# Moving stores behind their data, and reweaving two product halves, in a hybrid RG-LRU and attention block

## The chip, the cores and the metric

The kernel runs on one core of one Trainium2 chip. The metric is device time in microseconds (us) of one execution. Five engines work side by side, each in the order in which its instructions were written: TensorE (PE, with its weight loads as PEld), VectorE (DVE), ScalarE (ACT), GpSimd (POOL) and SyncE (SP), which here only issues transfers between DRAM and the on-chip memory (SBUF).

## The reference

One encoder block on x of 256 tokens by 2048 channels, in float32:

```python
xn = rms_norm(x, norm_pre_w)
z = xn @ w_in                        # 2048 x 13312
u_lru, g_lru, q, k, v, g_attn, m_lru, m_attn = split(z)
u = centred_depthwise_conv(u_lru)    # width 4
h = rg_lru(u, forward) + rg_lru(u, backward)   # gates of 128x128 blocks, then a scan over tokens
y_a = h * silu(g_lru)
y_b = windowed_gqa(rope(q), rope(k), v, sink) * silu(g_attn)
merged = sigmoid(m_lru) * (y_a @ w_proj_a) + sigmoid(m_attn) * (y_b @ w_proj_b)
out = x + rms_norm(merged @ w_out, norm_post_w)
```

## The kernel before

All weights are read once from one packed DRAM tensor, `wall`, in rows of 1 MB (128 partitions by 2048 floats). Each row is turned into two rounded pieces, a high one `wh` (a cast on ACT, L217) and the rest `wl` (a subtraction on DVE, L219), and each product is made of three matmuls on PE: high by high, high by low, low by high.

**Steps.** Three strings (START, MERGE, OUT) write out by hand the order in which rows are used. In START, `g`, `h`, `w`, `k` are blocks: `g2.0` is a row of the gates of branch A (tile `gl`), `h` of branch B (`ga`), `w` of the LRU's input (`u`), `k` of the keys, and two rows make one result. A name with `m`, such as `Lm6.0`, is a part of a product that is computed in Strassen's manner with seven products instead of eight: L and M are the two halves of the merge gate `m_lru`, and this document calls them the two gate halves. Time in the program is counted in half steps: a block takes two, a part one. START has 140 half steps. Index expressions such as `at(T, fn)` or `soon(fn, d)` put work at half step T, or d half steps from now, into every engine's order.

**What is loaded when.** `fetch` runs at the start of each step. A block's row (and the rows of `m2`) goes into a ring of three `raw` tiles, three steps ahead, by a load on SP (L205). The parts `m1`, `m5`, `m6`, `m4` of one half share two cells x of two tiles each (`Lx0a` and so on): the first is loaded and the others are added into it by accumulating loads on POOL (L190), five steps ahead; `m3` and `m7` share the cells y, and the first load of x or y goes through SP (L192), four steps ahead. A part with a sum of x as its other operand also loads that sum, 512 KB, four steps ahead (`x_sum`, L335, tile `Lm` or `Mm`). The LRU's own gate weights come four half steps ahead of each pair of blocks (L627). A block's or a part's row is split into `wh` and `wl` two steps ahead of its matmuls.

**What is put away.** SBUF doesn't hold all. It is cut into 45 tiles of 512 KB, the `units`, from which weights' pieces, LRU tiles, cells, sums and results are all drawn; a new tile waits until the last instruction on the one that it replaces is done, and the one that was given back longest ago is taken first. So results that are needed only later are stored to DRAM by `park` (L787) and read back by `back` (L791): the sigmoid gates `tm` (of L and M), the silu gates `sga`, the first branch's results `ya`, the second's `yb` and the first product `pa`. The eight groups of sums of x are computed at half steps 18, 22, ... 46 (`x_sums`) and stored too (L330, DRAM tensor `away`).

All of these stores and nearly all loads stand in one order, SP's. SP waits at each transfer until the data are there (a store), or until the place is free (a load); everything behind it in SP's order stands too. Before, the stores stand 2 or 3 half steps behind the instruction that makes their data.

Of the kernel before, what the change touches and what calls it, by code (L numbers as in the profile page):

```python
# [59 lines left out]
    o3.2 o3.3""".split()  # L60

START = """u0.0 u0.1 u0.2 u0.3 v0.0 v0.1 v0.2 v0.3 g0.0 g0.1 h0.0 h0.1 w4.0 w4.1 g2.0 g2.1 h2.0 h2.1 w6.0 w6.1 g4.0 g4.1
    Lm1.0 h4.0 h4.1 Lm1.1 w8.0 Lm2.0 w8.1 Lm2.1 g6.0 Lm5.0 g6.1 Lm5.1 h6.0 h6.1 Lm3.0 w10.0 Lm3.1 w10.1 Lm6.0 g8.0
    Lm6.1 g8.1 Lm7.0 h8.0 h8.1 Lm7.1 w12.0 Lm4.0 w12.1 Lm4.1 g10.0 Mm1.0 g10.1 Mm1.1 h10.0 h10.1 Mm2.0 w14.0 Mm2.1
    w14.1 Mm5.0 g12.0 Mm5.1 g12.1 Mm3.0 h12.0 h12.1 Mm3.1 g14.0 Mm6.0 g14.1 Mm6.1 h14.0 Mm7.0 h14.1 Mm7.1 k0.0 k0.1
    Mm4.0 k2.0 Mm4.1 k2.1""".split()
XSUM = (18, 22, 26, 30, 34, 38, 42, 46)
LRU = (-4, 0, 2, 2, 2, 2, 2, 4)
QUADS = {"u": ("w_in", U0), "v": ("w_in", V0), "p": ("w_proj_a", 0), "a": ("w_in", MA0),
# [44 lines left out]
def body(ctx, tc, x, xT, wall, wlru, pvec, npost, ident_d, mask_d, rope_d, out):  # L114
# [9 lines left out]
    def unit(name, dt=F32, shape=(P, 4, S)):  # L124
        return units.tile(list(shape), dt, tag="u", name=name)

    def bank(name, shape=(P, 2, S)):
        return psum.tile(list(shape), F32, tag="bg", name=name, bufs=4)
# [4 lines left out]
    def half_unit(name, tag, dt=F32, bufs=2):  # L133
        return small.tile([P, 2, S], dt, tag=tag, name=name, bufs=bufs)
# [10 lines left out]
    def parts_of(h, l, src):  # L145
        nc.scalar.copy(h, src)  # L146
        soon(lambda: nc.vector.tensor_tensor(l, src, h.bitcast(F32), ALU.subtract))
# [12 lines left out]
    def at(hs, fn):  # L160
        assert hs >= now[0], (hs, now[0])
        due.setdefault(hs, []).append(fn)
# [9 lines left out]
    def soon(fn, d=1):  # L172
        at(now[0] + d, fn)
# [127 lines left out]
    def sums_of(name, src, done, f=None):  # L301
        a = src.rearrange("p a b -> p (a b)")
        a11, a12, a21 = (a[:, i * P:(i + 1) * P] for i in (0, 2, 1))
        ends = src.rearrange("p a (b c) -> p (a b) c", b=2)[:, 0:4:3]
        psum = f is None
        f = (half_unit(f"{name}f", "uu", F32) if psum else f).rearrange("p a (b c) -> p (a b) c", b=2)
        t = unit(name, F32R, (P, 4, 2, P))

        def make(a21):
            nc.vector.tensor_tensor(f[:, 0:2], ends, a21.unsqueeze(1).to_broadcast([P, 2, P]), ALU.subtract)  # L310
            nc.vector.scalar_tensor_tensor(f[:, 2], f[:, 1], -1.0, a11, ALU.mult, ALU.subtract)
            nc.vector.scalar_tensor_tensor(f[:, 3], f[:, 2], -1.0, a12, ALU.mult, ALU.subtract)
            soon(lambda: parts_of(t[:, :, 0], t[:, :, 1], f))
            done(t)

        if psum:

            nc.scalar.copy(f[:, 3], a21)
            soon(lambda: make(f[:, 3]))
        else:  # L320
            make(a21)
# [5 lines left out]
    def x_sums(n):  # L327
        v = unit(f"xa{n}")
        nc.vector.tensor_tensor(v[:, 0:2], xs[n][:, :, 0].bitcast(F32), xs[n][:, :, 1].bitcast(F32), ALU.add)
        store = lambda t: nc.sync.dma_start(away[n // 4][:, :, n % 4], t.rearrange("p a b c -> p a (b c)").bitcast(F32))  # L330
        sums_of(f"xx{n}", v[:, 0:2], lambda t: soon(lambda: store(t), 3), v[:, 2:4])

    def x_sum(name, s, q):
        t = unit(name, F32R, (P, 4, 2, P))
# [283 lines left out]
    sgl, sga = [], []  # L618
    ya, yb = [None] * 8, [None] * 8

    def lru_pair(n, b):

        v = {}
# [67 lines left out]
        def gate_out():  # L691
            h = v["gr"]
            y = sgl[n // 4][:, n % 4:n % 4 + 2]
            nc.vector.tensor_tensor(h[:, 0:2], h[:, 0:2], h[:, 2:4], ALU.add)
            nc.vector.tensor_tensor(y, h[:, 0:2], y, ALU.mult)
            v.clear()
            if n in (2, 6, 10):
                soon(lambda: park("ya", sgl, n // 4), 2)
            elif n > 10:
                soon(lambda: y_parts(n // 2))  # L700

# [14 lines left out]
    def y_parts(q):  # L716
        ya[q] = pair_unit(f"ya{q}")
        n = q % 2 * 2
        parts_of(ya[q][:, :, 0], ya[q][:, :, 1], sgl[q // 2][:, n:n + 2])

    def silu_evac(units_list, n):
        def done(ps):
            if n % 4 == 0:
                units_list.append(unit(f"sg{n}"))
            dst = units_list[n // 4][:, n % 4:n % 4 + 2]

            def sigmoid():
                sg = half_unit(f"sig{n}", "p")
                nc.scalar.activation(sg, dst, AF.Sigmoid)
                soon(lambda: nc.vector.tensor_tensor(dst, dst, sg, ALU.mult))  # L730
                if units_list is sga and n % 4 == 2:
                    soon(lambda: park("sga", sga, n // 4), 3)

            scaled(dst, ps, lambda: soon(sigmoid))
        return done

    tm, sm, ms, msum = {}, {}, {}, {}
# [6 lines left out]

    def gated_out(gates, c, t):
        if t == 1 and gates is tm:
            soon(lambda: park("tm", tm, c), 2)

    def gate_evac(gates, c):
        def done(t, ps):  # L750
# [31 lines left out]
    def park(key, store, c):  # L782

        d = parked[key, c] = dram.tile([P, 1024], F32, name=f"park{key}{c}")
        t = store[c]
        store[c] = None
        nc.sync.dma_start(d, flat(t))  # L787
# [58 lines left out]
    def head(hd, qh, ql, b, both):  # L846

        g, j = hd // 4, hd % 4
        sk = pv[:, PV_SINK + hd:PV_SINK + hd + 1]
        ts = [slice(t * P, (t + 1) * P) for t in range(2)]  # L850
        v = {}

        def scores():
            v["sc"] = bank(f"sc{hd}")
            for t in range(2):
                mm3(v["sc"][:, t], qh[:, j, ts[t]], ql[:, j, ts[t]], kv["kh"][:, g], kv["kl"][:, g], True, True)

        def expo():
            p = v["p"] = half_unit(f"p{hd}", "p")
            sc = v.pop("sc")  # L860
            m, nm, es = tiny(f"m{hd}"), tiny(f"nm{hd}"), tiny(f"es{hd}")
            dn = v["dn"] = tiny(f"dn{hd}")
            for t in range(2):
                nc.vector.tensor_tensor_reduce(p[:, t], sc[:, t], table["mask"][:, t], rtok_sc[:, t:t + 1], sk, ALU.add, ALU.max, m[:, t:t + 1])  # L864
            nc.vector.tensor_scalar(nm, m, -1.0, None, ALU.mult)
            soon(lambda: exps(p, nm, es, dn))

        def exps(p, nm, es, dn):
            for t in range(2):
                nc.scalar.activation(p[:, t], p[:, t], AF.Exp, bias=nm[:, t:t + 1], accum_out=dn[:, t:t + 1])  # L870
            nc.scalar.activation(es, nm, AF.Exp, bias=sk)
            v["es"] = es

        def normalise():
            dn, rd = v["dn"], tiny(f"rd{hd}")
            nc.vector.tensor_tensor(dn, dn, v["es"], ALU.add)
            nc.vector.reciprocal(rd, dn)
            soon(lambda: [nc.scalar.activation(v["p"][:, t], v["p"][:, t], AF.Copy, scale=rd[:, t:t + 1]) for t in range(2)])

        def flip():  # L880
            v["pt"] = bank(f"pt{hd}")
            for kt in range(2):
                for t in range(2):
                    nc.tensor.transpose(v["pt"][:, kt, ts[t]], v["p"][:, t, ts[kt]], ident)  # L884

        def p_parts():
            if j % 2 == 0:
                both.update({s: unit(f"p{s}{hd}", F32R, (P, 2, 2, S)) for s in "hl"})
            parts_of(both["h"][:, :, j % 2], both["l"][:, :, j % 2], v.pop("pt"))
            v.clear()  # L890

        def values():
            both["o"] = bank(f"o{hd}")
            ks = slice(g * P, (g + 1) * P)
            for kt in range(2):
                mm3(both["o"], kv["vh"][:, kt, ks], kv["vl"][:, kt, ks], both["h"][:, kt], both["l"][:, kt], kt == 0, kt == 1)

        def gate_out():
            y = sga[g][:, j - 1:j + 1]
            nc.vector.tensor_tensor(y, both["o"], y, ALU.mult)  # L900
            both.clear()
            if j == 3 and g < 3:
                soon(lambda: park("yb", sga, g), 2)

        for d, fn in ((0, scores), (1, expo), (3, normalise), (5, flip), (6, p_parts)):
            at(b + d, fn)
        if j % 2 == 1:
            at(b + 10, values)
            at(b + 11, gate_out)
# [17 lines left out]
    def add_pa(c):  # L927
        def done(t, ps):
            nc.vector.tensor_tensor(tm[c][:, t], ps, tm[c][:, t], ALU.mult)
            if t == 1:  # L930
                soon(lambda: park("pa", tm, c), 2)

        add_rows(f"pa{c}_", ya, done)

# [94 lines left out]
    b, n = ticks(), ticks(len(plan))  # L1029
# [159 lines left out]
```

## Time and profile before

| | |
|---|---|
| median of 3 runs | 894.74 us (894.59 to 894.96) |
| the profiled execution | 894.17 us, of which 892.2 us from the first instruction to the last |
| DVE busy | 714.1 us (80%) |
| ACT busy | 611.6 us (69%) |
| POOL busy | 58.6 us (7%) |
| transfers | 235.13 MB, mean 264 GB/s |
| SP's queue, POOL's queue | 60.0% and 19.5% of the 16 DMA engines' time |
| granted TensorE clock | 0.998 |

The profile is one execution. An engine's busy time is the union of its instructions; a matmul's end is modelled, and the next one starts before it. "Releaser" is what ended a wait. A store or load is seen twice: when SP (or POOL) issues it, and when its data have landed. The DMA share of a window can read a little over 1.

### The profile page before, as it was taken

What the parts mean: (1) busy time and instruction counts of PE and PEld (TensorE: products, weight loads), DVE (VectorE), ACT (ScalarE), POOL (GpSimd) and SP (SyncE); (2) the same over time, 40 slices, a digit from 0 to 9 for tenths busy, and PEclk for the clock granted to TensorE, in tenths of its full rate; (3) what the DMA queues carried; (4) which work ended last, traced back from release to release, by engine and by line L of the source; (5) the groups of instructions that cost most, each with busy time, mean ns of one, the idle gap of its engine ahead of it and who ended that gap; (6) DMA issues with size and microseconds to landing.
All of it is one profiled execution on the core that took longest, in us unless ns stands there. A gap on an engine that the chain in (4) does not pass through costs nothing.

```text
span 892.2 us, 12273 instructions
## 1 busy us (share of the span) xinstructions
PE 879.0 (99%) x4566; PEld 753.0 (84%) x4566; DVE 714.1 (80%) x974; ACT 611.6 (69%) x885; POOL 58.6 (7%) x88
## 2 busy tenths in 40 slices
PE   9999999999899999999999999999999999999996
PEld 8888888888688888888888888888888888888885
DVE  6899999898697987898987768576676776687776
ACT  7689697869688795998554565455587654455754
POOL 0000000011001011100000000000101100000200
PEclk9999999999999999999999999999999999999999
DMA  9757689899859989965867556556999997799972
GB/s 337 261 189 265 221 290 302 292 330 288 299 195 316 314 260 321 315 212 203 313 231 259 189 189 218 188 208 239 303 327 333 304 289 255 276 316 387 230 181 95
DMA packets 51420, 235.13 MB, mean 264 GB/s; under 512 B 5377, under 2 KB 10241, under 8 KB 35105
## 3 DMA queue, kind: packets, MB, share of 16 engines
q1 hardware_dynamic: 41568, 200.03, 60.0%
q0 software_dynamic: 9216, 33.56, 19.5%
q10 hardware_dynamic: 576, 0.76, 0.3%
q8 instruction: 36, 0.59, 0.3%
q14 instruction: 24, 0.19, 0.1%
HBM read 218.60 MB, written 15.73 MB: 263 GB/s over the span
## 4 chain that ended last, share of the span: by engine, by line
PE 72%; DVE 9%; DMA 9%; issue 5%; ACT 3%; POOLq 0%; ACTq 0%; SPq 0%; DVEq 0%; POOL 0%
DMA raw<-wall_dram 9%; PE q L250 7%; DVE wl L219 5%; PE q L248 3%; PE ga L250 3%; PE gl L250 3%; PE k L250 2%; PE u L250 2%; PE ga L248 2%; ACT wh L217 2%; PE gl L248 2%; PE Am L225 1%; PE Am L223 1%; PE Am L224 1%; PE u_ps L540 1%
## 5 line engine op out<-in xcount | busy, mean ns | idle before, releaser
L219 DVE TENSOR_TENSOR wl<-raw,wh 128x1024 fp32r<-128x1024 f32 (+1 forms) x264 | 311.7, 1201 | 49.1 <-ACT wh L217 42.7
L217 ACT CAST wh<-raw 128x1024 fp32r<-128x1024 f32 (+1 forms) x263 | 264.7, 1037 | 57.6 <-DMA raw<-wall_dram 44.5
L250 PE MATMUL gl<-xs,wh 128*128 128x512 f32 x256 | 63.5, 391 | 2.3 <-ACT wh L217 2.3
L250 PE MATMUL ga<-xs,wh 128*128 128x512 f32 x256 | 63.5, 391 | 0.0
L250 PE MATMUL q<-xs,wh 128*128 128x512 f32 x256 | 62.8, 391 | 0.0
L250 PEld LDWEIGHTS gl<-xs,wh 128*128 128x128 f32 x256 | 46.9, 188 | 11.7 <-ACT wh L217 2.7
L250 PEld LDWEIGHTS ga<-xs,wh 128*128 128x128 f32 x256 | 46.7, 188 | 8.8
L250 PEld LDWEIGHTS q<-xs,wh 128*128 128x128 f32 x256 | 46.6, 188 | 8.8
L146 ACT CAST ph<-pt 128x512 fp32r<-128x512 f32 x16 | 9.4, 588 | 61.9 <-PE pt L884 61.9
L250 PE MATMUL u<-xs,wh 128*128 128x512 f32 x192 | 47.5, 391 | 0.0
L250 PEld LDWEIGHTS u<-xs,wh 128*128 128x128 f32 x192 | 35.2, 188 | 6.7
L248 PEld LDWEIGHTS ga<-xs,wl 128*128 128x128 f32 x256 | 32.9, 191 | 3.0 <-DVE wl L219 1.9
L248 PE MATMUL ga<-xs,wl 128*128 128x256 f32 x256 | 33.9, 283 | 1.3 <-DVE wl L219 1.3
L248 PE MATMUL q<-xs,wl 128*128 128x256 f32 x256 | 34.4, 284 | 0.0
L248 PEld LDWEIGHTS q<-xs,wl 128*128 128x128 f32 x256 | 33.1, 191 | 1.2
L248 PEld LDWEIGHTS gl<-xs,wl 128*128 128x128 f32 x256 | 32.8, 191 | 1.3
L248 PE MATMUL gl<-xs,wl 128*128 128x256 f32 x256 | 33.2, 283 | 0.0
L864 DVE CUSTOM_DVE_ANT_0 p<-sc,table,pv 128x256 f32<-128x256 f32 x32 | 16.1, 541 | 19.9 <-PE sc L225 19.9
L248 PEld LDWEIGHTS u<-xs,wl 128*128 128x128 f32 x192 | 24.6, 191 | 0.9
L248 PE MATMUL u<-xs,wl 128*128 128x256 f32 x192 | 24.9, 283 | 0.0
L645 DVE SCALAR_TENSOR_TENSOR uu<-upad,pv,uu 128x256 f32<-128x256 f32 x48 | 23.2, 483 | 1.7
L146 ACT CAST ms<-mt 128x512 fp32r<-128x512 f32 x8 | 4.7, 588 | 24.2 <-PE mt L950 24.2
(524 smaller groups left out, 2256.6 us busy)
## 6 DMA issues: line engine op xcount, KB each, us to landing
raw<-wall_dram SPq DMA_DIRECT2D x127, 1024.0 KB, 6.4
lraw<-wlru_dram SPq DMA_DIRECT2D x8, 512.0 KB, 5.8
away<-xx SPq DMA_DIRECT2D x8, 512.0 KB, 3.7
Lm<-away SPq DMA_DIRECT2D x8, 512.0 KB, 16.9
Mm<-away SPq DMA_DIRECT2D x8, 512.0 KB, 15.1
Am<-away SPq DMA_DIRECT2D x8, 512.0 KB, 10.1
raw<-wall_dram SPq DMA_DIRECT2D x8, 256.0 KB, 4.7
parksga<-sg SPq DMA_DIRECT2D x4, 512.0 KB, 4.7
```

What stands on the lines that cost most here:

```text
L146: nc.scalar.copy(h, src)
L217: cast(hs, raw)
L219: nc.vector.tensor_tensor(ls, raw, hs.bitcast(F32), ALU.subtract)
L223: nc.tensor.matmul(ps, wh, xh, start=start, stop=False, skip_group_check=more)
L224: nc.tensor.matmul(ps, wh, xl, start=False, stop=False, skip_group_check=more)
L225: nc.tensor.matmul(ps, wl, xh, start=False, stop=stop, skip_group_check=more)
L248: nc.tensor.matmul(ps[:, 1], wl[:, sl], a[:, 0], start=False, stop=False)
L250: nc.tensor.matmul(ps, wh[:, sl], a, start=k == 0, stop=k == KT - 1)
L540: nc.tensor.matmul(ups[b // 2][:, b % 2, m], w[:, sl], a[:, n], start=k == 0 and w is wh and m == 0, stop=stop)
L645: nc.vector.scalar_tensor_tensor(u, up[:, j, tap:tap + S], cw[:, tap:tap + 1], u, ALU.mult, ALU.add)
L864: nc.vector.tensor_tensor_reduce(p[:, t], sc[:, t], table["mask"][:, t], rtok_sc[:, t:t + 1], sk, ALU.add, ALU.max, m[:, t:t + 1])
```

## The change

Two things. First, the stores are issued later, counted in half steps behind their data: sums of x 3 becomes 7, `ya` 2 becomes 7, `sga` 3 becomes 7, `tm` 2 becomes 5, `yb` and `pa` 2 become 4. Nothing is added or taken away. Second, in START the parts of L and M are moved by one block here and there. Counted in half steps from the start, all blocks from `h6.0` on begin at the same half step or one earlier, and all parts from `Lm5.1` on at the same or two later (`Mm7.1`: four later). For example `Lm6.0 g8.0 Lm6.1 g8.1 Lm7.0 h8.0` (half steps 72 to 79) becomes `Lm6.0 g8.0 g8.1 Lm6.1 h8.0 Lm7.0` (72 to 80). Since `fetch` goes by steps and the LRU's work by the half step of its `g` block, those move along.

```diff
@@ START
-    Lm1.0 h4.0 h4.1 Lm1.1 w8.0 Lm2.0 w8.1 Lm2.1 g6.0 Lm5.0 g6.1 Lm5.1 h6.0 h6.1 Lm3.0 w10.0 Lm3.1 w10.1 Lm6.0 g8.0
-    Lm6.1 g8.1 Lm7.0 h8.0 h8.1 Lm7.1 w12.0 Lm4.0 w12.1 Lm4.1 g10.0 Mm1.0 g10.1 Mm1.1 h10.0 h10.1 Mm2.0 w14.0 Mm2.1
-    w14.1 Mm5.0 g12.0 Mm5.1 g12.1 Mm3.0 h12.0 h12.1 Mm3.1 g14.0 Mm6.0 g14.1 Mm6.1 h14.0 Mm7.0 h14.1 Mm7.1 k0.0 k0.1
-    Mm4.0 k2.0 Mm4.1 k2.1""".split()
+    Lm1.0 h4.0 h4.1 Lm1.1 w8.0 Lm2.0 w8.1 Lm2.1 g6.0 Lm5.0 g6.1 h6.0 Lm5.1 h6.1 Lm3.0 w10.0 Lm3.1 w10.1 Lm6.0 g8.0
+    g8.1 Lm6.1 h8.0 Lm7.0 h8.1 Lm7.1 w12.0 Lm4.0 w12.1 g10.0 Lm4.1 g10.1 Mm1.0 h10.0 Mm1.1 h10.1 Mm2.0 w14.0 w14.1
+    Mm2.1 g12.0 Mm5.0 g12.1 Mm5.1 h12.0 Mm3.0 h12.1 g14.0 Mm3.1 g14.1 Mm6.0 h14.0 Mm6.1 h14.1 Mm7.0 k0.0 k0.1 Mm7.1
+    k2.0 Mm4.0 k2.1 Mm4.1""".split()
@@ x_sums
-        sums_of(f"xx{n}", v[:, 0:2], lambda t: soon(lambda: store(t), 3), v[:, 2:4])
+        sums_of(f"xx{n}", v[:, 0:2], lambda t: soon(lambda: store(t), 7), v[:, 2:4])
@@ lru_pair, gate_out
-                soon(lambda: park("ya", sgl, n // 4), 2)
+                soon(lambda: park("ya", sgl, n // 4), 7)
@@ silu_evac
-                    soon(lambda: park("sga", sga, n // 4), 3)
+                    soon(lambda: park("sga", sga, n // 4), 7)
@@ gated_out
-            soon(lambda: park("tm", tm, c), 2)
+            soon(lambda: park("tm", tm, c), 5)
@@ head, gate_out
-                soon(lambda: park("yb", sga, g), 2)
+                soon(lambda: park("yb", sga, g), 4)
@@ add_pa
-                soon(lambda: park("pa", tm, c), 2)
+                soon(lambda: park("pa", tm, c), 4)
```

## The prediction

> **What bounds the kernel now.** I read the page first, for the engine that is nearly full.
>
> ```profile
> PE 879.0 (99%) x4566; PEld 753.0 (84%) x4566; DVE 714.1 (80%) x974; ACT 611.6 (69%) x885; POOL 58.6 (7%) x88
> ```
>
> TensorE is busy for 99% of the 892.2 us span, and the change gives it the same matmuls, only in another order. So a gain can only come from the moments when PE stands still, and a loss only from new ones. The view of waits, for PE alone, names them all:
>
> ```profile
> PE gl L250 <- ACT wh L217: 2.3, 1, 2.3
> PE ga L248 <- DVE wl L219: 1.3, 2, 1.1
> ...
> PE gate L223 <- ACT gi L669: 0.6, 1, 0.6
> ```
>
> What is left out stands in the first 20 us, ahead of all that is changed. PE's timeline shows where the first two rows lie:
>
> ```profile
> 226.68 0.39 PE L223 MATMUL Lm<-wh,Lm 128*128 128x512 f32 x1
> ...
> 228.94 0.39 PE L224 MATMUL Lm<-wl,Lm 128*128 128x512 f32 x1
> 229.17 0.39 PE L225 MATMUL Lm<-wh,Lm 128*128 128x512 f32 x1
> 231.85 2.12 PE L250 MATMUL gl<-xs,wh 128*128 128x512 f32 x8 [2.29 <-ACT wh L217]
> ...
> 240.28 1.97 PE L250 MATMUL ga<-xs,wh 128*128 128x512 f32 x8
> 242.46 1.22 PE L248 MATMUL ga<-xs,wl 128*128 128x256 f32 x8 [0.21 <-DVE wl L219]
> 244.73 1.21 PE L248 MATMUL ga<-xs,wl 128*128 128x256 f32 x8 [1.05 <-DVE wl L219]
> ```
>
> By the order of START these are `Lm6.1` (226.68), `g8.1` (231.85), `Lm7.0`, and `h8.0` (240.28). A matmul is shown with 0.39 us, but the next one starts 0.23 after it: modelled ends hide 0.16 us of each wait. The four waits are thus 2.29 + 0.21 + 1.05 + 0.6 = 4.15 us as shown and 4.15 + 4 x 0.16 = **4.8 us** by starts. That is the most that the change can bring. ACT's timeline tells what they waited for:
>
> ```profile
> 230.75 2.00 ACT L217 CAST wh<-raw 128x1024 fp32r<-128x1024 f32 x2 [7.25 <-DMA raw<-wall_dram]
> ...
> 237.69 1.06 ACT L217 CAST wh<-raw 128x1024 fp32r<-128x1024 f32 x1 [1.59 <-DMA raw<-wall_dram]
> ```
>
> The weights of `g8.1` landed at 230.7 and those of `h8.0` at 237.7; ACT had stood idle for 7.25 and 1.59 us. The waits on DVE at 242 and 244 are what that delay left on ACT and DVE. So I went to the transfers, by stretches:
>
> ```profile
> 170.00:175.00 5.00, 5.00 (x31) 4.45 (x31) 4.43 (x6) 4.42 (x5) 0.87 (x1) 1.00 0.41 106
> 175.00:240.00 65.00, 62.71 (x340) 54.22 (x339) 52.51 (x61) 46.97 (x64) 9.70 (x13) 1.00 1.04 314
> 310.00:315.00 5.00, 5.00 (x32) 4.43 (x31) 4.96 (x8) 4.98 (x9) 0.00 (x0) 1.00 0.42 164
> 320.00:385.00 65.00, 64.39 (x352) 55.83 (x351) 55.00 (x65) 53.43 (x70) 9.28 (x11) 1.00 1.04 313
> ```
>
> The last two columns are the DMA share and GB/s. From 175 to 240 us and from 320 to 385 the DMA engines are full, at 314 GB/s; just ahead of each stretch they are idle for more than half of 5 us. SP's timeline and its waits (window 160 to 180) show why:
>
> ```profile
> 164.06 0.33 SPq L205 DMA_DIRECT2D raw<-wall_dram  x1
> 173.08 0.33 SPq L787 DMA_DIRECT2D parkya<-sg  x1
> 173.50 0.41 SPq L205 DMA_DIRECT2D raw<-wall_dram  x1
> ```
>
> ```profile
> SPq L787 <- DVE sg L695: 8.7, 1, 8.7
> ```
>
> SP stood for 8.7 us at the store of `ya`, whose data DVE made only at 173; the next weights stood behind it. The second gap is the same with `sga`:
>
> ```profile
> 307.80 0.33 SPq L627 DMA_DIRECT2D lraw<-wlru_dram  x1
> 314.54 0.33 SPq L787 DMA_DIRECT2D parksga<-sg  x1
> ```
>
> **The change, part by part.** *The stores of `ya` and `sga`, five and four half steps later.* The row behind the first gap, that of `h6.1`, takes the ring place of `g6.0`, which was free when DVE had split it:
>
> ```profile
> 167.18 1.23 DVE L219 TENSOR_TENSOR wl<-raw,wh 128x1024 fp32r<-128x1024 f32 x1 [1.94 <-ACT wh L217]
> ```
>
> At 168.4 us, so its 1 MB can go 5.1 us earlier. It needs 1.05 MB / 314 GB/s = 3.3 us of transfer, and the gap offers 0.59 x 5 = 2.95 us. All that follows in the full stretch then lands 2.95 us earlier. The second gap offers 0.58 x 5 = 2.9 us to the stretch after 320. The store itself comes behind its data by more than SP ever waited for it, and costs no wait of its own.
>
> *The weave around half step 75.* SP issued in this order before:
>
> ```profile
> 193.82 0.33 SPq L205 DMA_DIRECT2D raw<-wall_dram  x1
> 201.98 0.33 SPq L335 DMA_DIRECT2D Lm<-away  x1
> 208.46 0.33 SPq L627 DMA_DIRECT2D lraw<-wlru_dram  x1
> 209.69 0.33 SPq L787 DMA_DIRECT2D parksga<-sg  x1
> 210.11 0.43 SPq L205 DMA_DIRECT2D raw<-wall_dram  x1
> 211.69 0.33 SPq L335 DMA_DIRECT2D Lm<-away  x1
> 212.11 7.96 SPq L205 DMA_DIRECT2D raw<-wall_dram  x2
> ```
>
> These are the rows of `g8.0` (193.82), the sum for `Lm6.1`, LRU weights, the store of `sga`, `g8.1` (210.11), the sum for `Lm7.0`, and `h8.0` with `h8.1` (212.11). The row of `g8.1` takes the place of `w10.0`, which DVE gave back at 201.3:
>
> ```profile
> 200.06 1.22 DVE L219 TENSOR_TENSOR wl<-raw,wh 128x1024 fp32r<-128x1024 f32 x1
> ```
>
> In the new order `fetch` asks for `g8.1` at half step 70, ahead of the sum for `Lm6.1` and of the other two, instead of at 72 behind all three. So it goes out at 201.3 instead of 210.1. With the same 230.7 - 210.1 = 20.6 us to landing it is there at 221.9 and cast at 223.0. PE needs it where `Lm6.1` was, at 226.7: 3.7 us in hand, and the 2.29 wait goes.
>
> What is late next is `h8.0`. Its new place: a part takes 229.17 + 0.23 - 226.68 = 2.72 us, a block 240.28 - 231.85 - 2.72 = 5.71 us, so `g8.1` and `Lm6.1` end at 226.68 + 5.71 + 2.72 = 235.1. A cast takes 1.06, so the row must land by 234.0, against 237.7 before: 3.7 us are wanted. To be had are the 2.95 us of the gap, and 1.67 us (0.52 MB / 314 GB/s) each for the store of `sga` and the sum for `Lm7.0`, which now stand behind this row on SP: 6.3 us in all, landing at 231.4. The bounds are 0 (order changes, the bytes don't) and 6.3; I take 6.3, since the gap is seen in the windows and the order follows from the code. Anything over 3.7 gives the same time. The DVE waits go along, for ACT and DVE are then not held up.
>
> *The weave around half step 118.* The gate wait came when ACT stood at the row of `g14.0`, as the chain of waits shows:
>
> ```profile
> 331.30 22.27 DMA raw<-wall_dram
> ```
>
> PE needs it one half step (2.7 us) sooner now. It gains the second gap's 2.9 us, and the first loads of the cells of `Mm3.1` with their sum (1.57 MB, 5.0 us) now go behind it instead of ahead of the rows before it; 5.2 us better in the balance, against a wait of 0.6 + 0.16. It goes; if not, 0.8 us remain.
>
> *The stores of the sums of x, `tm`, `yb` and `pa`.* SP's waits and the table of transfers:
>
> ```profile
> SPq L330 <- DVE xx L147: 39.6, 8, 8.5
> ```
>
> ```profile
> parktm<-mg SPq DMA_DIRECT2D x4, 512.0 KB, 4.4
> ```
>
> Some 5 us of SP's time per store of sums go, but PE had no wait in that stretch, so nothing is gained there. Two reads come closer behind their stores: the sum for `Lm5.1` three half steps (8.2 us) behind the last store of sums, and `tm` for `p0` two (5.4 us). The stores land in about 4.4 us, so SP stands little or not at all; what queues behind it are weights for which three ring tiles are filled ahead. I take nothing; the other end is the 1 to 2 us by which a slow landing would hold SP.
>
> *Longer use of SBUF.* Each store holds one of the 45 units for two to five half steps more, and a unit is wanted for every quarter of a block, 5.71 / 4 = 1.4 us. A load can wait for one, as the sum at 201.98 did for 7.8 us:
>
> ```profile
> SPq L335 <- PE gate L225: 8.1, 2, 7.8
> ```
>
> Such a load would then wait up to 1.4 us more, or 2.8 with two stores held at once. I take 0, since `g8.1` no longer stands behind such a load, and keep 2.8 for the range. The Trainium skill speaks against this part: "Perfetto Trace Analysis", Identifying Performance Opportunities, says that recurring gaps on the engine that should be full can mean that SBUF has no room for the next tile, and by that rule holding tiles longer lengthens the gaps. The trace bears it out only in part, since ACT's 7.25 us were ended by a DMA; what it would cost is the second rival.
>
> **The sum.** 4.8 us of waits go and nothing comes: the profiled execution's 894.17 us (892.2 of span, 2.0 around it) become 889.4. The median of the runs is 0.57 above that execution, so 894.74 - 4.8 = **889.9 us**. A measurement of this kernel can tell 0.2%, 1.8 us, from no change.
>
> **Rivals.** *Full engines stay full.* From 175 to 240 us the DMA share is 1.04, and what is issued earlier could only wait longer. For it: `h8.0` took 25.6 us to land. Against it: the 41% just before. Then `g8.1` is in time, but `h8.0` still lands at 237.7, is cast at 238.75, 3.6 us after its new place; with the DVE waits (0.21 + 1.05 + 0.32) and the gate's 0.8 the waits are 6.0 instead of 4.8 us: 895.9. The Trainium skill has the ground for this, too: "DMA: Bandwidth & Descriptors", Issuing engines are not separate DMA queues, says that all queues run on the same 16 engines.
>
> *SBUF runs short, and the kernel gets slower.* The delayed `sga` and `ya` hold units in this very stretch; SP stands longer at the sum and the LRU weights ahead of `h8.0`, which is asked for 2.8 us later and lands at 240.5. It is 6.4 us late for a place that moved forward; with 1.6 and 0.8 as above the waits are 8.8 us: 898.7. It decides from where the row of `h8.0` lands later than 238.2 (waits of 4.8 + 1.8, less 1.6 and 0.8, are 4.2 us behind 235.1, less the cast). For it: SP did stand for a unit here. Against it: one or two units are few of 45.
>
> *Half of it.* `g8.1` is in time, `h8.0` and the gate keep their waits (2.5 us): 892.4, still faster.
>
> **How the numbers follow.** Chances: the forecast 0.60, half of it 0.10, full engines 0.14, SBUF short 0.16. That gives faster 0.70, within 0.2% 0.14, slower 0.16. The range goes from all 5 us gained and a little noise, 889.0, to the rival with full engines, 895.9; outside are the slower case and little else.
>
> **What would show it.** Right: no store of `ya` or `sga` that SP waits for; a DMA share near 1 at 170 to 175 us; `g8.1` issued near 201 us; PE's waits after 100 us near 0. Wrong: an ACT wait on a raw row of `h8.0` or `g14.0` with a PE wait behind it; SP blanks on L335, L627 or L192 that end with a PE instruction and are longer than before; a PE wait at a half step where there was none, above all behind 420 us, where `tm` is read back.

## The result and the profile after

The change took 894.85 us (median of 4 runs, 894.59 to 895.53) to 889.44 us (4 runs, 888.86 to 889.65): a ratio of 0.9937, with a 95% interval of 0.9920 to 0.9955. The profiled execution took 889.43 us, with a span of 887.1 us. The granted TensorE clock reads 0.998 in both profiled executions, so it is not what differs.

The first block of the page and its chain of work that ended last (before, the chain was 72% PE, 9% DVE and 9% DMA):

```profile
PE 877.8 (99%) x4566; PEld 753.3 (85%) x4566; DVE 713.3 (80%) x974; ACT 610.4 (69%) x885; POOL 58.6 (7%) x88
```

```profile
PE 97%; DMA 2%; DVE 0%; ACT 0%; DVEq 0%; issue 0%; ACTq 0%
```

The view of waits for PE, whole (what it waited for, total, times, longest):

```profile
PE spin L444 <- POOL eps L440: 1.0, 1, 1.0
PE u_ps L540 <- DVE xs L471: 0.8, 1, 0.8
```

Both stand in the first 20 us. After that the view shows no wait of PE any more. The span is 5.1 us shorter: PE's idle time fell from 892.2 - 879.0 = 13.2 to 887.1 - 877.8 = 9.3 us, and its busy time by 1.2 us with the same 4566 matmuls. Of this 1.2 the modelled ends explain 0.65 by the prediction's 0.16 for each of the four waits; where the rest lies is not shown.

The windows that showed the gaps, now of the changed kernel (the second number is PE's busy time; the last three are granted clock, DMA share, GB/s):

```profile
170.00:175.00 5.00, 5.00 (x30) 4.42 (x29) 3.65 (x5) 4.46 (x5) 0.87 (x1) 1.00 1.00 419
175.00:240.00 65.00, 65.00 (x361) 56.80 (x360) 59.22 (x70) 52.73 (x70) 9.84 (x15) 1.00 1.04 313
310.00:315.00 5.00, 5.00 (x31) 4.45 (x30) 4.96 (x6) 4.64 (x7) 0.00 (x0) 1.00 0.78 274
```

The first gap is closed (0.41 to 1.00), the second half closed (0.42 to 0.78). In the stretch to 240 us the DMA engines moved as much as before, 313 GB/s, yet PE is busy for all 65.00 us instead of 62.71. SP's timeline of the changed kernel:

```profile
166.61 0.33 SPq L335 DMA_DIRECT2D Lm<-away  x1
169.24 0.33 SPq L205 DMA_DIRECT2D raw<-wall_dram  x1
...
185.94 0.42 SPq L787 DMA_DIRECT2D parkya<-sg  x1
...
210.24 0.33 SPq L205 DMA_DIRECT2D raw<-wall_dram  x1
215.16 0.33 SPq L335 DMA_DIRECT2D Lm<-away  x1
215.53 0.49 SPq L787 DMA_DIRECT2D parksga<-sg  x1
```

The row of `h6.1` goes out at 169.24 (before 173.50); `ya` is stored at 185.94, without a wait; `h8.0` goes out at 210.24 (before at 212.11 or after), ahead of the sum for `Lm7.0` and the store of `sga`. `g8.1` went out at 202.08 and landed at 213.97. ACT's timeline shows when `h8.0` came, and POOL's when the added cells of `Lm4.1` were asked for, before (the second fence) and after (the third):

```profile
226.61 1.05 ACT L217 CAST wh<-raw 128x1024 fp32r<-128x1024 f32 x1 [0.40 <-DMA raw<-wall_dram]
```

```profile
221.84 0.86 POOL L190 DMA_DIRECT2D Lx1a<-wall_dram  x1 [5.44 <-DVE wl L219]
```

```profile
226.43 0.86 POOL L190 DMA_DIRECT2D Lx1a<-wall_dram  x1 [8.98 <-DVE wl L219]
```

`h8.0` landed at 226.5, 11.1 us earlier than before. One part of this stands in no step of the prediction: POOL issues its adding loads (1 MB for `Lm4.1`) when DVE has split the cells they follow, and that now comes 4.6 us later, so they no longer run beside this row. What each part is worth is worked out below, under `h8.0`.

### The profile page after: what moved, and what is told of

It reads as the page before. It is cut to its first block, busy times and chain, and to the rows that moved or that the text cites. A ratio compares the mean times of both kernels' runs of the same rounds, so it can differ in the third digit from the quotient of the medians.

```text
span 887.1 us, 12275 instructions
## 1 busy us (share of the span) xinstructions
PE 877.8 (99%) x4566; PEld 753.3 (85%) x4566; DVE 713.3 (80%) x974; ACT 610.4 (69%) x885; POOL 58.6 (7%) x88
## 4 chain that ended last, share of the span: by engine, by line
PE 97%; DMA 2%; DVE 0%; ACT 0%; DVEq 0%; issue 0%; ACTq 0%
PE q L250 7%; PE ga L250 7%; PE gl L250 7%; PE u L250 5%; PE ga L248 3%; PE gl L248 3%; PE q L248 3%; PE u L248 3%; PE k L250 2%; PE Am L225 1%; PE Am L223 1%; PE Lm L223 1%; PE Mm L223 1%; PE Lm L224 1%; PE Am L224 1%; PE Mm L224 1%
```

## The experiments

What was to be explained: that the waits went at all, through which part, and why `h8.0` came so much earlier. Theory A is the prediction's: SP stands at stores whose data aren't made, and the rows behind come late; the filled gap and the better place in SP's order together bring them in time. Theory B: the place in the order does it all, and with full engines an earlier store gains nothing. The SBUF theory: units held longer make SP wait longer for a free one. The medians of the kernel before, taken anew beside each set of runs, lie between 894.17 and 894.85, so differences of a few tenths between two experiments say nothing. Diffs are against the kernel before unless it is said otherwise.

**The stores alone** (all six `soon` lines of the change, START as before):

```diff
-        sums_of(f"xx{n}", v[:, 0:2], lambda t: soon(lambda: store(t), 3), v[:, 2:4])
+        sums_of(f"xx{n}", v[:, 0:2], lambda t: soon(lambda: store(t), 7), v[:, 2:4])
...
-                soon(lambda: park("pa", tm, c), 2)
+                soon(lambda: park("pa", tm, c), 4)
```

> START as before, all stores as late as in the change. Theory A (SP's stand at the stores of ya and sga left the DMA engines idle just ahead of the full stretches; the weave only adds slack): the row of g8.1 goes out about 209 us, lands near 226 and is cast by 227.5 against 229.4 needed; h8.0 lands near 233 against 236.8; no PE wait after 100 us; about 890 us, ratio 0.995. Theory B (the weave does it, by asking for g8.1 ahead of the sum, and the engines being full an earlier issue alone gains nothing): all four waits stay, about 895 us, ratio 0.999 to 1.000. SBUF theory (units held longer lengthen SP's waits for a unit): slower than before, 896 us or more.

889.46 us, ratio 0.9949 (0.9933 to 0.9965): all of the gain that can be told from the full change. Its window, and ACT at the row of `h8.0`:

```profile
170.00:175.00 5.00, 5.00 (x31) 4.46 (x30) 3.92 (x5) 4.43 (x6) 0.87 (x1) 1.00 0.90 358
```

```profile
233.38 1.05 ACT L217 CAST wh<-raw 128x1024 fp32r<-128x1024 f32 x1 [3.03 <-DMA raw<-wall_dram]
```

`h8.0` came 237.7 - 233.4 = 4.3 us earlier, and PE has no wait after the first 20 us; B is out. The 4.3 us are not the gap's alone: the store of `sga`, which went out ahead of this row before (209.69), now goes out behind it (212.67) and lands after it. The run with `ya` alone, below, has only the gap in it.

**The weave alone** (the stores as before, START as after):

```diff
-    Lm6.1 g8.1 Lm7.0 h8.0 h8.1 Lm7.1 w12.0 Lm4.0 w12.1 Lm4.1 g10.0
+    g8.1 Lm6.1 h8.0 Lm7.0 h8.1 Lm7.1 w12.0 Lm4.0 w12.1 g10.0 Lm4.1
...
```

> START as in the change, all stores as early as before. Theory A: SP still stands about 8 us at the store of ya, the DMA share at 170 to 175 us stays below 0.6; g8.1 goes out near 201 and is in time, but h8.0 has only the sum behind it, lands near 236.0 against 234.0 needed: waits of 2 to 3.6 us remain, 892 to 893.5 us, ratio 0.997 to 0.9985. Theory B: no wait remains, about 890 us, ratio 0.994 to 0.995.

890.37 us, 0.9955 (0.9938 to 0.9972): faster than expected, about as good as the stores. The gap at 170 stayed, so this gain is not that gap's:

```profile
170.00:175.00 5.00, 5.00 (x28) 4.34 (x27) 3.51 (x4) 4.61 (x6) 0.88 (x1) 1.00 0.42 130
```

```profile
226.95 0.86 POOL L190 DMA_DIRECT2D Lx1a<-wall_dram  x1 [9.61 <-DVE wl L219]
```

```profile
232.61 1.05 ACT L217 CAST wh<-raw 128x1024 fp32r<-128x1024 f32 x1 [5.87 <-DMA raw<-wall_dram]
```

POOL's adds come 5.1 us later than before, here too, and `h8.0` lands at 232.5, where 236.0 was expected: of the two transfers of the forecast only the sum for `Lm7.0` went behind this row, since the store of `sga` still goes out ahead of it (210.33, the row 211.59). PE is left with 0.2 us (`gate` on `ul`). The two parts give 0.9949 and 0.9955 alone and 0.9937 together: the gains are not added, since each alone makes the rows nearly punctual.

**Two entries moved** (stores as before, of the weave only `g8.1` ahead of `Lm6.1` and `h8.0` ahead of `Lm7.0`):

```diff
-    Lm6.1 g8.1 Lm7.0 h8.0 h8.1 Lm7.1 w12.0
+    g8.1 Lm6.1 h8.0 Lm7.0 h8.1 Lm7.1 w12.0
```

> All stores as early as before; of the weave only two moves, g8.1 ahead of Lm6.1 and h8.0 ahead of Lm7.0. Theory: the row of g8.1 goes out near 202 us, and the cell adds of POOL that wait for Lm6.1 come some 4 us later and so behind the row of h8.0; the waits at g8.1 and h8.0 go, the gate's 0.8 us at 355 us stay: about 890.5 us, ratio 0.9955. If the whole weave is needed: 892 us or more.

891.08 us, 0.9965 (0.9953 to 0.9977). `g8.1` goes out at 201.61, `h8.0` lands at 232.3, with the gap at 170 as open as before (0.41). Two swaps around half step 75 thus carry most of what the whole weave gives, with 0.5 us left at `ga` and 0.2 at `gate`.

**The stores of `ya` and `sga` alone (the diff below), then the four others without these two, then `ya` and `sga` each by itself:**

```diff
-                soon(lambda: park("ya", sgl, n // 4), 2)
+                soon(lambda: park("ya", sgl, n // 4), 7)
-                    soon(lambda: park("sga", sga, n // 4), 3)
+                    soon(lambda: park("sga", sga, n // 4), 7)
```

> START as before, only the stores of ya and sga later (7 and 7). Theory A: as with all stores later, about 890 us, ratio 0.995, for these two are the ones that SP stood at ahead of the full stretches. Theory B: about 895 us.

889.85 us, 0.9951 (0.9936 to 0.9966), no PE wait after the start, and both gaps closed (1.02 and 1.02). These two lines are the store part. `h8.0` landed at 230.4 here, 3 us ahead of the run with all stores late, whose order around this row is the same: the landing of one row in one execution is good to a few us only.

> START as before, only the stores of the sums of x, tm, yb and pa later (7, 5, 4, 4). Theory A: SP waits about 40 us less in total at the stores of sums, but no PE wait goes: 895 us, ratio 1.000, within 0.1%. SBUF theory: the sums' units held longer make it 1 to 3 us slower.

894.6 us, 1.0006 (0.9995 to 1.0017; 10 runs): the stores of the sums, `tm`, `yb` and `pa` bring nothing, as the prediction took it. SP no longer waits for DVE at the store of the sums, but it waits at the read behind it instead, it still stands at the store of `ya` till 173.17, and `gl` at `g8.1` keeps PE waiting, as before:

```profile
SPq L335 <- DMA away<-xx: 5.0, 1, 5.0
```

```profile
PE gl L250 <- ACT wh L217: 3.3, 1, 3.3
```

> START as before, only the stores of ya later (7). Theory A (the gap at 170 to 175 us, left by SP's stand at the store of ya, is what makes the weights of g8.1 and h8.0 late): rows land 2.9 us sooner, g8.1 near 227.8 (cast by 228.9, needed at 229.4), h8.0 near 234.7 (needed by 236.8); these waits go, the gate's 0.8 us stay: about 890.5 us, ratio 0.9955. If instead the store of sga ahead of the row of g8.1 matters most, 2 us or more of wait stay here: 892.5 us.

891.48 us, 0.9965 (0.9954 to 0.9975; 10 runs), 1 us short of what was expected. The gap at 170 is filled to 0.90, `h8.0` lands 2.3 us earlier (235.4) with the store of `sga` still ahead of it, and the four waits of before are gone; but a new one has come. ACT, then PE at the row of `h8.0` and at the LRU gate:

```profile
235.39 1.05 ACT L217 CAST wh<-raw 128x1024 fp32r<-128x1024 f32 x1 [3.37 <-DMA raw<-wall_dram]
236.35 1.05 ACT L146 CAST lwh<-lraw 128x1024 fp32r<-128x1024 f32 x1
237.29 1.05 ACT L217 CAST wh<-raw 128x1024 fp32r<-128x1024 f32 x1
238.25 0.61 ACT L146 CAST ul<-uu 128x512 fp32r<-128x512 f32 x1
...
241.27 2.00 ACT L217 CAST wh<-raw 128x1024 fp32r<-128x1024 f32 x2
```

```profile
237.90 1.98 PE L250 MATMUL ga<-xs,wh 128*128 128x512 f32 x8
...
245.40 0.39 PE L224 MATMUL gate<-ul,lwh 128*128 128x256 f32 x1 [1.57 <-DVE ul L147]
```

```profile
242.35 1.23 DVE L219 TENSOR_TENSOR wl<-raw,wh 128x1024 fp32r<-128x1024 f32 x1 [1.76 <-ACT wh L217]
...
244.68 0.67 DVE L147 TENSOR_TENSOR ul<-uu,ul 128x512 fp32r<-128x512 f32 x1
```

The cast of `h8.0` ends at 236.4, 1.5 us before PE uses it at 237.90: in time. But ACT works in order and had stood 3.37 us for that row, so its next casts are late, DVE waits 1.76 us for one of them, and `ul`, which DVE makes behind that, keeps PE waiting 1.57 us at 245.40. The chain of waits that ends there runs back through these rows to this landing. With the row at 233.4 (the stores alone) this wait does not come.

> START as before, only the stores of sga later (7). Theory A: the gap at 170 to 175 us stays, the row of g8.1 goes out 1.2 us sooner with 1.7 us less ahead of it and lands near 228 to 229: a wait of 0 to 0.9 us stays at g8.1, none at h8.0; the gap at 310 to 315 us fills and the gate's wait goes: 889.8 to 890.8 us, ratio 0.995 to 0.996. If only the gap at 170 to 175 us counts: waits of 3 to 4 us stay, about 893.5 us.

892.11 us, 0.9979 (0.9969 to 0.9989; 10 runs): less than expected. `h8.0` lands at 235.1 and the same kind of wait is left, 0.9 us at `gate` on `ul` and 0.6 at `ga` on `wl`. The two stores together end these leftovers.

**The stores earlier than before**, one half step behind the data:

```diff
-                soon(lambda: park("ya", sgl, n // 4), 2)
+                soon(lambda: park("ya", sgl, n // 4), 1)
-                    soon(lambda: park("sga", sga, n // 4), 3)
+                    soon(lambda: park("sga", sga, n // 4), 1)
```

> START as before, the stores of ya and sga earlier than before (1 half step behind their data instead of 2 and 3). Theory A: the row of h6.0, too, now stands behind the store of ya until 173 us; the DMA engines are idle some 3 us more ahead of the full stretch, the rows of g8.1 and h8.0 land 3 us later: 897 to 898 us, ratio 1.003 to 1.004. If SP's stand there doesn't set PE's waits: 894.5 us, ratio 1.000.

896.1 us, 1.0021 (1.0011 to 1.0030; 10 runs): slower, the direction expected but 1.6 us by the medians instead of 3 (the profiled execution took 897.7). SP stood from 162 to 174 and the gap is empty:

```profile
161.67 0.38 SPq L335 DMA_DIRECT2D Lm<-away  x1
174.43 0.33 SPq L787 DMA_DIRECT2D parkya<-sg  x1
```

```profile
170.00:175.00 5.00, 5.00 (x29) 4.34 (x29) 3.12 (x4) 4.98 (x6) 0.88 (x1) 1.00 0.02 6
```

**More transfers in the full stretch.** A copy from DRAM to DRAM that nothing reads (1 MB) is issued on SP at half step 60, in the kernel before and in the changed one:

```diff
+    extra = dram.tile([P, 2048], F32, name="extra")
+    at(60, lambda: nc.sync.dma_start(extra, wall[0]))
```

> The kernel before with one transfer more: 1 MB copied from the packed weights to an unused DRAM tile, issued by SP at half step 60, at the start of the full stretch; its result is not used. Theory (the bytes ahead of g8.1 and h8.0 set PE's waits, one us of transfer is one us of wait): 1.05 MB / 314 GB/s = 3.3 us more, about 897.8 us, ratio 1.0037; more if a copy within DRAM moves slower. If the engines' being full doesn't set the waits: 894.5 us.

> The change with the same transfer more, 1 MB from DRAM to DRAM at half step 60, its result not used. Theory: the row of h8.0, landed at 226.5 us, lands near 230, still ahead of the 233.4 at which the kernel with late stores alone showed no wait: the copy is hidden, 889.5 us, ratio 0.994 to 0.995. If the change had left no time in hand: 892.5 us or more.

Before with the copy: 895.71 us, 1.0017 (1.0007 to 1.0027; 10 runs), 1.5 us more than the 894.17 beside it, half of the 3.3 expected. The profiled execution took 894.38, only 0.2 more than that of the kernel before, so its trace does not show where the 1.5 us lie. Changed with the copy: 889.31 us, 0.9949 (0.9934 to 0.9964), no PE wait after the first 20 us; `h8.0` lands at 229.7. So the changed kernel has time in hand for 1 MB more, and the kernel before had none; but a microsecond of transfers is not a microsecond of waits: in that trace one of POOL's adds came at 217.70 instead of 212.47, and `h8.0` landed at 238.4 instead of 237.7.

**The stores later still** (against the changed kernel; `tm`, `yb` and `pa` go to 6):

```diff
-        sums_of(f"xx{n}", v[:, 0:2], lambda t: soon(lambda: store(t), 7), v[:, 2:4])
+        sums_of(f"xx{n}", v[:, 0:2], lambda t: soon(lambda: store(t), 9), v[:, 2:4])
-                soon(lambda: park("ya", sgl, n // 4), 7)
+                soon(lambda: park("ya", sgl, n // 4), 12)
-                    soon(lambda: park("sga", sga, n // 4), 7)
+                    soon(lambda: park("sga", sga, n // 4), 12)
...
```

> The change with all stores later still: sums of x 9, ya and sga 12, tm, yb and pa 6 half steps behind their data. Theory A: what counts is only that SP no longer stands at a store; nothing more to gain and nothing lost, 889.5 us, ratio 0.994 to 0.995, no PE wait after 100 us. SBUF theory (each half step longer in a unit lengthens SP's waits for a free unit): waits come back, 891 us or more.

890.37 us, 0.9959 (0.9944 to 0.9974). A PE wait of 0.5 us comes back, at 180 us. SP's longest wait at 160 to 176 us, then SP's timeline, ACT and PE:

```profile
SPq L335 <- DMA away<-xx: 6.9, 1, 6.9
```

```profile
154.57 0.47 SPq L787 DMA_DIRECT2D parksga<-sg  x1
155.09 0.53 SPq L330 DMA_DIRECT2D away<-xx  x1
157.79 0.33 SPq L205 DMA_DIRECT2D raw<-wall_dram  x1
```

```profile
165.90 1.05 ACT L217 CAST wh<-raw 128x1024 fp32r<-128x1024 f32 x1 [3.19 <-DMA raw<-wall_dram]
```

```profile
180.28 0.50 PE L224 MATMUL Lm<-wl,Lm 128*128 128x512 f32 x1 [0.50 <-DVE wl L219]
```

The sum for `Lm5.1` is read right behind its own store, and SP stands 6.9 us, until 172.7, for the store to land. PE's wait does not come from this, though. Followed back, it goes through DVE's and ACT's order to the row cast at 165.90: ACT had stood 3.19 us for it, 2.07 in the changed kernel. SP issued this row at 157.79, before it stood, but right behind the store of `sga` and one of the sums; that these made it late is argued from the order. With the stores of the sums back at 7 and the rest as late:

```diff
-        sums_of(f"xx{n}", v[:, 0:2], lambda t: soon(lambda: store(t), 9), v[:, 2:4])
+        sums_of(f"xx{n}", v[:, 0:2], lambda t: soon(lambda: store(t), 7), v[:, 2:4])
```

> As the run with all stores later still, but with the sums of x at 7 as in the change; ya and sga 12, tm, yb and pa 6. If its 0.5 us of PE wait at 180 us came from the sum of Lm5.1, whose load stood 6.9 us for the landing of the last store of sums: the wait is gone, 889.4 us, ratio 0.994 to 0.995. If it came from units of SBUF held longer: the wait and about 890.4 us stay.

889.1 us, 0.9952 (0.9936 to 0.9969); the store of the sums now goes out behind that row, SP's wait at the read is 1.2 us, and PE's wait 0.2. The two intervals overlap, so the times alone do not tell these two kernels apart. Holding `ya` and `sga` for 12 half steps costs nothing that can be told. This is no better than the change: no kernel tried is clearly faster, and by PE's waits there is nothing left for such edits to win.

## Why the prediction was right

Forecast was 889.9 us, measured 889.44; by the profiled executions 4.8 us less were forecast and 894.17 - 889.43 = 4.74 came. By the medians it is 894.85 - 889.44 = 5.4, the median of the kernel before being uncertain by some 0.7. That the total fits says little of the parts: it is the sum of PE's waits, the most that could be won, and once the rows are in time no error in how early they come shows in it.

*The four waits.* All gone. By the trace's sums 3.9 us of idle time and 1.2 us of busy time went, against 4.15 of waits and 0.65 of hidden ends. This division is only as good as the modelled ends.

*SP's stand makes the gap, and the gap makes the rows late.* Right, and shown both ways: the two stores later close the gaps and remove the waits (0.9951), the two stores earlier empty the gap to 0.02 and add some (1.0021). `ya` alone, which fills the first gap and changes nothing next to `h8.0`, brought that row 2.3 us earlier, where 2.95 were forecast. The row behind the first gap was put at 168.4 and went out at 169.24.

*`g8.1`.* Put at 201.3, went out at 202.08. It landed at 213.97 instead of 221.9: 11.9 us after its issue, not 20.6. Carrying over the time to landing was too careful. With the new order but the gap open it took 17.7 us (the weave alone) and 18.1 (two moves), and in the changed kernel with 1 MB more on SP's queue ahead of it 18.7: so the time to landing hangs on what is still under way ahead of the row, and most of the gain came with the stores.

*`h8.0`.* The step that was mis-sized. 6.3 us of earlier landing were forecast and 11.1 came. The sum counted the gap and two transfers on SP's queue; it left out POOL's adds, which moved from ahead of this row's landing to behind it. The DMA view counts what each queue moved from 170 us to this landing, packets and MB (q1 is SP's, q0 POOL's), before (170 to 237.67) and after (170 to 226.53):

```profile
q1 hardware_dynamic: 2736, 13.64, 52.2%
q0 software_dynamic: 1728, 6.29, 47.1%
```

```profile
q1 hardware_dynamic: 2595, 12.79, 58.1%
q0 software_dynamic: 1391, 5.11, 45.4%
```

At 313 GB/s the 1.18 MB less on POOL's queue are an estimated 3.8 us and the 0.85 MB less on SP's 2.7, against nothing and 3.3 in the forecast; the remaining 4.6 us are left for the gap, against 2.95. The weave alone agrees: with the gap open the row gained 5.2 us, of which the sum for `Lm7.0` is 1.7, and POOL's queue had moved 0.82 MB less. No run held back the adds and nothing else, so their share stays an estimate.

*The deadline of that row.* Judged by when PE uses it, 234.0, and that was too lax a rule: with `ya` alone the row was in time for its matmul by 1.5 us, and PE still lost 1.57 us to `ul`, made behind it in ACT's and DVE's order. In the changed kernel it does not matter, for the row came 7.5 us before the forecast deadline.

*The sum of two parts.* The prediction built one sum out of stores and weave and did not say that either would nearly do. Its rival "half of it" (892.4) is near what one store alone gives (891.48, 892.11), but those kernels are left with a wait on `ul` that it did not name. Its 2.5 us of waits left are 2.3 by the prediction's own figures, since the 2.29 us that go hide 0.16 more.

*The gate at 355 us.* It went although the second gap closed only to 0.78. But it also went with the two moves alone, which change nothing near it and leave that gap at 0.53, and with `ya` alone (0.69). So neither of the causes forecast for it, 2.9 and 5.0 us, was needed, and that this term came true is in part luck. Why so little was enough to end it stays open.

*The other stores.* Nothing, as taken. Behind the store of the sums SP waits 1.9 us at a read, the forecast's other end of 1 to 2 us; it costs nothing here, and no PE wait could be traced to the 6.9 us of it with the stores later still either.

*Full engines.* This rival was wrong. The stretch is as full as before, 1.04, and the row that was waited for still came earlier, since others went behind it; the copy in the changed kernel is hidden. In the kernel before, with nothing in hand, 1 MB more did cost 1.5 us.

*SBUF short.* Its first half happened: all SP's waits at reads of sums (L335) that end with a matmul add up to 57.6 us before and 68.5 after. Those on a matmul of `Lm` or `gate` grew from 2.3 + 8.1 us (before, the first row here and the one in the prediction) to 12.5 + 3.3 us (after),

```profile
SPq L335 <- PE Lm L225: 2.3, 2, 1.2
```

```profile
SPq L335 <- PE Lm L225: 12.5, 3, 6.8
...
SPq L335 <- PE gate L225: 3.3, 1, 3.3
```

but the view shows no PE wait that follows from it. The total is some 70 us with the stores alone and some 54 with the weave alone, so it grew with the stores; whether because units are held longer or because SP asks sooner, no run separated. The Trainium skill has it that recurring gaps on the full engine can mean a lack of SBUF ("Perfetto Trace Analysis", Identifying Performance Opportunities). That was not the cause here: holding `ya` and `sga` for twelve half steps gave 0.9952, with 0.2 us of PE wait.

## What to carry to other kernels

A DMA queue that issues in order is a place where a store can cost a load: look for the stretch where the transfers idle just ahead of a stretch where they are full, and see what the issuing engine stood for. Put a store several steps behind its data, but see what it then stands next to: a read of the same DRAM tile right behind it waits for it to land, and an urgent load right behind it comes later. Put urgent loads ahead of those that can wait, and count the transfers of the other queues too. Take the deadline of a load from the in-order engine that works on it first, for what stands behind it there may be needed sooner than the load itself.

## What was not expected of the hardware

Stores that SP did not stand for land later. The page's table of transfers, before and after (KB each, median us from issue to landing):

```profile
away<-xx SPq DMA_DIRECT2D x8, 512.0 KB, 3.7
```

```profile
away<-xx SPq DMA_DIRECT2D x8, 512.0 KB, 8.5
```

These stores go out between 66 and 158 us, ahead of the full stretch. Before, five of the eight found at most 0.8 us of other transfers still to land when they went out, since SP had just stood for their data; after, each found one that took 5.5 us more or longer. With these stores late and those of `ya` and `sga` as before it is 8.7 us; that the transfers ahead are the reason was not tested by itself. A read three half steps behind such a store still waited 1.9 us for it, one two half steps behind 5.0, and one a single half step behind 6.9 us. And 1 MB more of transfers in a full stretch cost 1.5 us, not the 3.3 us that it would take at 314 GB/s, while one adding load, whose issue hangs on DVE, went out 5.2 us later; that these loads gave way is argued from that row of one execution, not tested by itself.
